# Output projection of block pairs in seven products instead of eight, with the branch projections as a stage of their own

## The chip, the core and the metric

The kernel runs on one core of a Trainium2 chip. The number that counts is the time of one execution on the device in microseconds; "before" is the median of three runs. Beside the runs there is one execution under the hardware profiler, from which all rows in this document come.

## What is computed

One encoder layer is applied to two sequences of 1024 tokens, x_prompt and x_sample, with shared weights and 1024 features. Sixteen learned meta tokens stand in front of each sequence as extra keys. Cut to what matters here:

```python
proj = h @ w_in                                   # queries, keys, values, gates of both branches
ya = window_attention(...) * silu(za)             # (tokens, 512)
yb = dense_attention(...) * silu(zb)              # (tokens, 512)
ua = ya @ w_ba                                    # (512, 1024)
ub = yb @ w_bb                                    # (512, 1024)
merged = sigmoid(ga) * ua + sigmoid(gb) * ub      # (tokens, 1024)
out = merged @ w_o                                # (1024, 1024)
y = layer_norm(ALPHA * h + out) * ln_g + ln_b
```

Everything is float32. The kernel gets there with a reduced format of TensorE: each operand is split into a rounded high part and the remainder, and a product is the sum of three matmuls, high by high, high by low and low by high.

## The kernel before

The 2048 tokens are 16 blocks of 128. The program runs in stages: keys, values and the first two gate columns; windowed attention; dense attention; the last two gate columns; and at the end one loop over the 16 blocks that does the branch projections, the merge, the output projection and the normalization. Attention outputs (`ysc`) and gates (`gsc`) lie in DRAM between the stages. The change touches the last loop and, a little, the gate stage ahead of it.

In that loop `branches(i)` multiplies the two attention outputs of block i with `wba` and `wbb`. `project` issues three matmuls of 128x512 for each 128 rows of a weight; a branch has 4 such rows and there are two column halves, so that is 48 matmuls. DVE multiplies each of the four results with its gate out of PSUM, POOL adds the two branches (`sg<-sg`), TensorE transposes the sum in 8 pieces of 128x128, ACT writes its high part (`mh`) and DVE its low part (`ml`). `finish(i - 1)` multiplies the previous block with `w_out`: 2 column halves, 8 rows each, 3 matmuls, so 48 again. DVE then adds ALPHA times the input (`xr<-xr,st`), takes `bn_stats` and `bn_aggr`, subtracts the mean and multiplies with the gain (`xr<-xr,mv,ln_gain`), computes the inverse root by nine tiny instructions on 128x1 tiles (`lny`, `lnh`, `lna`) and scales and shifts each half (`xr<-xr,lny,ln_bias`). Two DMAs write the block out.

What sets the order: every instruction is recorded by `Plan.record`, priced by `Plan.price` and put in order by `Plan.issue`, which takes for each engine the ready instruction with the lowest key. The prices and the delays between engines are one number per instruction and pair of engines; nothing in them makes one engine's instruction longer because another engine is at work. Each engine then runs its list strictly in that order and waits where an input is late. All DMAs stand in one queue, SP's. Since all instructions are issued in `Plan.issue`, all rows of the profile have line 278, and the tile's name tells what is what. PSUM has 8 banks of 128x512, given out in rings by tag: `sx` 3, `st` 2, `pj`, `o` and `tr` one each.

Of the kernel before, what the change touches and what calls it, by code (L numbers as in the profile page):

```python
# [282 lines left out]
def encoder(ctx, tc, d, out):  # L283
# [591 lines left out]
    raw = []
    wg = [load_weight(wp, w_in(GATE[2 + i]), KT, f"w{i}", (None, ptt)[WSUB[2 + i]]) for i in range(2)]
    x = kept_x(0)
    for i in range(2 * NT):
        nx = kept_x(i + 1) if i + 1 < 2 * NT else None
        for c in range(2):  # L880
            if i <= GSPLIT:
                gates(x, i, 2 + c, wg[c], ("pj", 1), wk, (ROPE_TAGS + (("rqs", 1),))[2 * i + c], raw)
            else:
                gates(x, i, 2 + c, wg[c], ("st", 2), wk)
        x = nx
        if i == GSPLIT:
# [6 lines left out]
            wd = pool("wd", 1, reuse_waits="tile")
            wk = pool("wk3", 2, reuse_waits="tile")
            stage = lambda: xp.tile([P, 4, P], F32, tag="xf", bufs=XF).rearrange("p c q -> p (c q)")
            wb = [weight(wd, d[n], 4, n) for n in ("wba", "wbb")]
            lnp = [wk.tile([P, D], F32, name=n, bufs=1) for n in ("ln_gain", "ln_bias")]
            pieces = [p for _, ps in wb for p in ps]
            wb = [u for u, _ in wb]
# [4 lines left out]
    for p in pieces:
        p()

    def load_y(i):
        y = x_tile()
        for b in range(2):
            load_x(ysc[b][i], y, 4 * b)  # L910
        sg = wk.tile([P, 4, 512], F32, tag="sg")
        for c in range(4):
            dma(sg[:, c], gsc[i][c])
        return y, sg

    y = load_y(0)
    wo = [load_weight(wp, d["w_out"][:, c * 512:(c + 1) * 512], KT, f"w{c}") for c in range(2)]
    for t, n in zip(lnp, ("ln_gain", "ln_bias")):
        dma(t, d[n].to_broadcast([P, D]))

    def branches(i, y, sg):

        mh, ml = (wk.tile([P, KT, P], F32R, tag="m" + e) for e in "hl")
        us = [bank("pj", 1), bank("o", 1), bank("sx", 3), bank("sx", 3)]
        for c in range(4):
            half, b = c // 2, c % 2
            project(us[c], [t[:, 4 * b:4 * b + 4] for t in y], wb[b], 4, half * 512, 512)
        for c in range(4):
            tt(out=sg[:, c], in0=us[c], in1=sg[:, c], op=ALU.mult)
        for half in range(2):  # L930
            m = sg[:, 2 * half]
            ptt(out=m, in0=m, in1=sg[:, 2 * half + 1], op=ALU.add)
            tr = bank("tr", 1) if half else bank("sx", 3)
            for c in range(4):
                nc.tensor.transpose(tr[:, c * P:(c + 1) * P], m[:, c * P:(c + 1) * P], ident)
            r = slice(4 * half, 4 * half + 4)
            tr = tr.rearrange("p (c q) -> p c q", c=4)
            act(mh[:, r], tr, AF.Copy)
            tt(out=ml[:, r], in0=tr, in1=mh[:, r].bitcast(F32), op=ALU.subtract)
        return mh, ml  # L940

    def finish(i, m):

        xr = wk.tile([P, D], F32, tag="xr")
        dma(xr, d["xtok"][i * P:(i + 1) * P])
        stats = wk.tile([P, 2, 6], F32, tag="stats")
        for c in range(2):
            pw = misc()
            project(pw, m, wo[c], KT, 0, 512)
            xc = xr[:, c * 512:(c + 1) * 512]  # L950
            nc.vector.scalar_tensor_tensor(out=xc, in0=xc, scalar=ALPHA, in1=pw, op0=ALU.mult, op1=ALU.add)
            nc.vector.bn_stats(out=stats[:, c], in_=xc)
        mv = wk.tile([P, 2], F32, tag="mv")
        nc.vector.bn_aggr(out=mv, in_=stats)
        nc.vector.tensor_scalar(out=mv[:, 1:2], in0=mv[:, 1:2], scalar1=1e-5, scalar2=None, op0=ALU.add)
        stt = nc.vector.scalar_tensor_tensor
        stt(out=xr, in0=xr, scalar=mv[:, 0:1], in1=lnp[0], op0=ALU.subtract, op1=ALU.mult)
        rstd = rsqrt(wk, mv[:, 1:2], 1, P, "ln")
        for c in range(2):
            cs = slice(c * 512, (c + 1) * 512)  # L960
            stt(out=xr[:, cs], in0=xr[:, cs], scalar=rstd, in1=lnp[1][:, cs], op0=ALU.mult, op1=ALU.add)
            dma(out[i // NT][0, (i % NT) * P:(i % NT + 1) * P, cs], xr[:, cs])

    done = None
    for i in range(2 * NT):
        m = branches(i, *y)
        if i + 1 < 2 * NT:
            y = load_y(i + 1)
        if i:
            finish(i - 1, done)  # L970
        done = m
    finish(2 * NT - 1, done)
# [44 lines left out]
```

## Time and profile before

| | us |
|---|---|
| median of 3 runs (lowest to highest) | 1812.28 (1812.25 to 1813.5) |
| the profiled execution's own time | 1811.3 |
| its span, first to last instruction | 1809.5 |
| TensorE (PE) busy | 1772.6 (98%) |
| VectorE (DVE) busy | 1149.9 (64%) |
| ScalarE (ACT) busy | 883.2 (49%) |
| GpSimd (POOL) busy | 249.8 (14%) |
| first matmul of the last loop starts at | 1430.35 |

All times in rows count from the span's start. "out<-in" gives the tile written and the tiles read; in a row of the timeline the second number is the duration, and "x2" merges two instructions that follow each other, whose joint time then stands there. PE busy is the time that matmuls were under way, and since they overlap, the distance from one start to the next is what one costs.

### The profile page before, as it was taken

To read this page: it belongs to the slowest core of one execution; us is meant where nothing else is said; L and a number is where in the kernel's file an instruction comes from. 1 tells how busy PE (TensorE), PEld (TensorE's weight loads), DVE (VectorE), ACT (ScalarE), POOL (GpSimd) and SP (SyncE) were. 2 spreads that over 40 slices of the span, in tenths; PEclk is the share of its full clock that TensorE was granted. 3 is DMA by queue.
4 is the path that set the end of the run, shared out by engine and by line. 5 is a ranking of instruction groups with operands and counts; after the bars stand their busy time and mean duration, and the time that the engine had idled before them with its cause. 6 is when DMAs were issued, how large, how long until landed. Compare 5 with 4: busy or idle time off the path is not lost. (4 is left out here: it accounts for less than half of the span.)

```text
span 1809.5 us, 26295 instructions
## 1 busy us (share of the span) xinstructions
PE 1772.6 (98%) x8954; PEld 1453.4 (80%) x8954; DVE 1149.9 (64%) x2908; ACT 883.2 (49%) x2265; POOL 249.8 (14%) x437
## 2 busy tenths in 40 slices
PE   7999999999999999999999999999999999999997
PEld 5778778888888778888888888877888878888886
DVE  7433334767677679888888888887200265555555
ACT  6222224666666667777777777788311220000000
POOL 2000002222221131111111111132000011111110
PEclk9999999999999999999999999999999999999999
DMA  9544445322223340100002000131654553333321
GB/s 338 215 161 163 141 145 182 124 92 91 95 96 99 103 143 32 56 30 33 30 33 76 30 33 30 41 103 59 241 180 155 186 169 117 117 117 116 111 71 47
DMA packets 111101, 199.09 MB, mean 110 GB/s; under 512 B 11814, under 2 KB 49894, under 8 KB 110966
## 3 DMA queue, kind: packets, MB, share of 16 engines
q1 hardware_dynamic: 110966, 197.40, 32.5%
q8 instruction: 71, 1.16, 0.3%
q14 instruction: 64, 0.52, 0.1%
HBM read 138.60 MB, written 58.75 MB: 109 GB/s over the span
## 5 line engine op out<-in xcount | busy, mean ns | idle before, releaser
L278 DVE TENSOR_TENSOR pl<-st,ph 116x512 fp32r<-116x512 f32 (+3 forms) x416 | 283.2, 684 | 56.1 <-ACT ph L278 52.1
L278 ACT ACTIVATE ph<-st 116x512 fp32r<-116x512 f32 (+3 forms) x416 | 248.1, 599 | 117.0 <-PE st L278 113.8
L278 PE MATMUL st<-ident,p 128*116 128x128 f32 (+2 forms) x1664 | 261.7, 272 | 6.4 <-ACT p L278 4.1
L278 PE MATMUL sx<-k,q 128*128 128x348 f32 (+3 forms) x1024 | 245.9, 340 | 5.2 <-ACT p L278 4.6
L278 PEld LDWEIGHTS st<-ident,p 128*116 128x116 f32 (+2 forms) x1664 | 200.8, 131 | 56.7 <-issue 7.7
L278 ACT ACTIVATE p<-sx,nb 128x348 f32<-128x348 f32 (+1 forms) x384 | 208.1, 552 | 56.1 <-DVE nb L278 55.9
L278 DVE TENSOR_REDUCE mn<-sx 128x1 f32<-128x348 f32 (+1 forms) x384 | 190.7, 511 | 34.4 <-PE sx L278 32.3
L278 PEld LDWEIGHTS sx<-k,q 128*128 128x128 f32 x1024 | 168.6, 189 | 34.5 <-ACT p L278 12.3
L278 PE MATMUL o<-ph,v 116*128 116x512 f32 (+3 forms) x416 | 179.3, 431 | 0.6 <-DVE yu L278 0.4
L278 ACT ACTIVATE xh<-xf 128x512 fp32r<-128x512 f32 x64 | 38.9, 626 | 287.8 <-PE sx L278 222.6
L278 PE MATMUL o<-pl,v 116*128 116x512 f32 (+3 forms) x416 | 167.0, 401 | 1.7 <-DVE pl L278 1.7
L278 DVE TENSOR_TENSOR xl<-xf,xh 128x512 fp32r<-128x512 f32 x64 | 57.2, 912 | 165.3 <-ACT xh L278 165.2
L278 PE MATMUL pj<-w0h,xh 128*128 128x512 f32 x272 | 112.9, 415 | 0.3 <-DVE z L278 0.3
L278 POOL TENSOR_TENSOR sg<-sg 128x512 f32<-128x512 f32 x32 | 46.2, 1445 | 469.0 <-DVE sg L278 276.2
L278 PE MATMUL pj<-w1h,xh 128*128 128x512 f32 x264 | 110.0, 417 | 0.5 <-DVE rope_rq L278 0.5
L278 PE MATMUL pj<-w0l,xh 128*128 128x512 f32 x272 | 107.9, 397 | 0.0
L278 PE MATMUL pj<-w1l,xh 128*128 128x512 f32 x264 | 107.3, 406 | 0.0
L278 PE MATMUL pj<-w0h,xl 128*128 128x512 f32 x272 | 107.0, 394 | 0.0
L278 PE MATMUL pj<-w1h,xl 128*128 128x512 f32 x264 | 106.4, 403 | 0.0
L278 ACT ACTIVATE q<-tr 64x256 fp32r<-64x256 f32 x256 | 96.4, 376 | 14.5 <-PE tr L278 11.8
L278 PEld LDWEIGHTS o<-pl,v 116*128 116x128 f32 (+3 forms) x416 | 78.8, 189 | 16.6 <-DVE pl L278 9.0
L278 PEld LDWEIGHTS o<-ph,v 116*128 116x128 f32 (+3 forms) x416 | 78.4, 188 | 14.5 <-ACT ph L278 5.4
(194 smaller groups left out, 3777.0 us busy)
## 6 DMA issues: line engine op xcount, KB each, us to landing
xh<-xsc SPq DMA_DIRECT2D x48, 512.0 KB
xl<-xsc SPq DMA_DIRECT2D x48, 512.0 KB
wf<-in_w_in_dram SPq DMA_DIRECT2D x64, 256.0 KB
gsc<-sg SPq DMA_DIRECT2D x64, 256.0 KB
sg<-gsc SPq DMA_DIRECT2D x64, 256.0 KB
xf<-in_xt_dram SPq DMA_DIRECT2D x32, 256.0 KB
xsc<-xh SPq DMA_DIRECT2D x16, 512.0 KB
xsc<-xl SPq DMA_DIRECT2D x16, 512.0 KB
```

What stands on the lines that cost most here:

```text
L278: getattr(op.eng.real, op.name)(*map(real, op.a), **{k: real(v) for k, v in op.k.items()})
```

## The change

The loop at the end becomes two stages.

The first stage goes over the 16 blocks twice, once for each half of the 1024 columns (`order`). `merge` does the two branch products of a block and a half (24 matmuls), multiplies with the gates, and adds the branches on DVE. `put_m`, two steps later, transposes the sum (4 pieces), copies it to SBUF unsplit and writes it to DRAM (`msc`). The attention outputs are read and split once for each half, so twice in all. Between these steps `operand` prepares seven combinations of the four quarters of `w_out` (quarters 11, 12, 21, 22 of 512x512): three quarters as they are and `t1 = 12 - 11`, `t2 = 22 - t1`, `t3 = 22 - 12`, `t4 = 21 - t2`. The differences are taken on POOL, and each result is split on ACT and DVE.

The second stage takes blocks in pairs, 2j and 2j + 1. Of the pair's merged block (2x2 pieces of 512 columns) `put` makes seven left operands: three pieces as they are and `s1 = 21 + 22`, `s3 = 11 - 21`, `s2 = s1 - 11`, `s4 = 12 - s2`, all four on POOL. Each operand is split: high part on ACT, low part on DVE, or on POOL for s2 and s4 (`SUBS`). `product` does one of the seven 512-deep products of a pair: 4 rows, 3 matmuls each, so 12 matmuls, and 84 for a pair where the loop before had 96. `put` runs `LEAD` = 4 products ahead. The products are put together on DVE (`e1`, `u2`, `u3`, `residual`), where `residual` also sums a row's values; `norm` takes the mean, lets ACT sum the squares, and scales and shifts on DVE. The seven products take seven of the eight PSUM banks in turn (`BANKS`). Gate tiles and other work tiles move to new rings (`raw`, 10 buffers; `xo`, 6).

TensorE has 768 matmuls of 128x512 less 96, so 672, in the output projection; the 768 of the branch projections and the 128 transposes stay as many.

```diff
+    def merge(h, y, sg):
+        us = [bank("sx", 3), bank("st", 2)]
+        for b in range(2):
+            project(us[b], [t[:, 4 * b:4 * b + 4] for t in y], wb[h][b], 4, 0, 512)
+            tt(out=sg[:, b], in0=us[b], in1=sg[:, b], op=ALU.mult)
+        m = sg[:, 0]
+        tt(out=m, in0=m, in1=sg[:, 1], op=ALU.add)
+        return m
...
+    def minus(x, y, o=None):
+        o = x if o is None else o
+        ptt(out=o, in0=x, in1=y, op=ALU.subtract)
+        return o
...
+    def put(o, n):
+        s = pairs[n]
+        if o == "11":
+            s.raw = {}
+            for q in ("11", "12", "21", "22"):
+                f = s.raw[q] = raw_tile()
+                r, c = int(q[0]) - 1, int(q[1]) - 1
+                dma(f, msc[2 * s.j + r][:, 4 * c:4 * c + 4])
+        f = s.raw
+        if o == "s3":
+            f["s1"] = raw_tile()
+            ptt(out=f["s1"], in0=f["21"], in1=f["22"], op=ALU.add)
+            f["s3"] = minus(f["11"], f["21"], f["21"])
+        elif o == "s2":
+            f["s2"] = minus(f["s1"], f["11"], f["11"])
+        elif o == "s4":
+            f["s4"] = minus(f["12"], f["s2"])
+        hl = wk.tile([P, 8, P], F32R, tag="xo", name="xo", bufs=XO)
+        act(hl[:, 0:4], f[o], AF.Copy)
+        (ptt if o in SUBS else tt)(out=hl[:, 4:8], in0=f[o], in1=hl[:, 0:4].bitcast(F32), op=ALU.subtract)
+        X[o, n] = hl[:, 0:4], hl[:, 4:8]
+
+    def product(o, n):
...
+        project(ps, X.pop((o, n)), (w_[:, 0:4], w_[:, 4:8]), 4, 0, 512)
+        if o == "11":
...
+            act(s.e1, ps, AF.Copy)
+        elif o == "12":
+            residual(s, 0, 0, ps, s.e1)
+        elif o == "s2":
+            s.u2, s.u3 = ev(), ev(False)
+            tt(out=s.u2, in0=ps, in1=s.e1, op=ALU.add)
+            tt(out=s.u3, in0=s.ps["s3"], in1=s.u2, op=ALU.add)
+        elif o == "22":
+            residual(s, 1, 0, ps, s.u3)
+        elif o == "s1":
+            tt(out=s.u2, in0=ps, in1=s.u2, op=ALU.add)
+            residual(s, 1, 1, ps, s.u3)
+            norm(s, 1)
+        elif o == "s4":
+            residual(s, 0, 1, ps, s.u2)
+            norm(s, 0)
+
+    def residual(s, r, c, src, more):
+        xc = flat(s.x[r][:, 4 * c:4 * c + 4])
+        nc.vector.scalar_tensor_tensor(out=xc, in0=xc, scalar=ALPHA, in1=src, op0=ALU.mult, op1=ALU.add)
+        nc.vector.tensor_tensor_reduce(out=xc, in0=xc, in1=more, op0=ALU.add, op1=ALU.add, scale=1.0, scalar=0.0,
+                                       accum_out=s.stats[r][:, c:c + 1])
+
+    def norm(s, r):
...
+        for c in range(2):
+            act(flat(raw_tile()), flat(xr[:, 4 * c:4 * c + 4]), AF.Square, bias=mv[:, 0:1], accum_out=sums[:, 2 + c:3 + c])
...
         rstd = rsqrt(wk, mv[:, 1:2], 1, P, "ln")
         for c in range(2):
             cs = slice(c * 512, (c + 1) * 512)
+            xc = flat(xr[:, 4 * c:4 * c + 4])
+            stt(out=xc, in0=xc, scalar=mv[:, 0:1], in1=lng[:, cs], op0=ALU.add, op1=ALU.mult)
+            stt(out=xc, in0=xc, scalar=rstd, in1=lnb[:, cs], op0=ALU.mult, op1=ALU.add)
```

How the lists of the engines read now, at two places. The first is POOL after the last attention step. Before, it has the 32 additions of the branches and nothing else, two for each block; the last five blocks:

```order
L278 TENSOR_TENSOR sg_18159<-sg_18159 128x512 x2
L278 TENSOR_TENSOR sg_18325<-sg_18325 128x512 x2
L278 TENSOR_TENSOR sg_18491<-sg_18491 128x512 x2
L278 TENSOR_TENSOR sg_18655<-sg_18655 128x512 x2
L278 TENSOR_TENSOR sg_18817<-sg_18817 128x512 x2
```

Now POOL has 28 differences for the weights in the first stage, and in the second stage, for each pair, these six instructions. They are shown for one pair in the middle, with buffer numbers; raw_19194 is s1, raw_19192 holds piece 21 and then s3, raw_19001 holds 11 and then s2, raw_19125 holds 12 and then s4:

```order
L280 TENSOR_TENSOR raw_19194<-raw_19192,raw_19193 128x512
L280 TENSOR_TENSOR raw_19192<-raw_19001,raw_19192 128x512
L280 TENSOR_TENSOR raw_19001<-raw_19194,raw_19001 128x512
L280 TENSOR_TENSOR raw_19125<-raw_19125,raw_19001 128x512
L280 TENSOR_TENSOR xo_19299<-raw_19001,xo_19299 128x512
L280 TENSOR_TENSOR xo_19386<-raw_19125,xo_19386 128x512
```

The additions `sg<-sg` moved to DVE, and six instructions of 128x512 for each pair of blocks took their place on POOL, where four stood for two blocks; each of the six has both inputs in SBUF.

The second place is DVE at the end of a block, and now at the end of a pair. Before, a block's mean, its inverse root and its last scaling stand like this, among the products with the gates:

```order
L278 SCALAR_TENSOR_TENSOR xr<-xr,st 128x512
L278 BN_STATS stats<-xr 128x6
L278 BN_AGGR mv<-stats 128x2
L278 TENSOR_SCALAR mv<-mv 128x1
L278 SCALAR_TENSOR_TENSOR xr<-xr,mv,ln_gain 128x1024
...
L278 TENSOR_SCALAR lny<-lny 128x1
L278 SCALAR_TENSOR_TENSOR lna<-lny,lnh 128x1
L278 SCALAR_TENSOR_TENSOR lny<-lna,lny 128x1
...
L278 SCALAR_TENSOR_TENSOR xr<-xr,lny,ln_bias 128x512 x2
L278 TENSOR_TENSOR sg<-o,sg 128x512
L278 TENSOR_TENSOR sg<-sx,sg 128x512 x2
L278 TENSOR_TENSOR ml<-sx,mh 128x512
```

Now (ISA is the instruction that adds and sums a row, and its read-out; xr_19082 is the pair's second block, xr_19111 its first, xr_19309 the next pair's first; raw_19199 and raw_19323 are pieces 11 and 12 of the pair after that; the last two rows are `u2` and `u3` of the next pair):

```order
L280 TENSOR_TENSOR xo_19406<-raw_19199,xo_19406 128x512
L280 SCALAR_TENSOR_TENSOR lny_19370<-lna_19377,lny_19370 128x1
...
L280 ISA xr_19309,stats0_19423<-xr_19309,ev_19364 128x512
...
L280 SCALAR_TENSOR_TENSOR xr_19082<-xr_19082,lny_19370,lnp_18368 128x512 x2
...
L280 TENSOR_TENSOR xo_19434<-raw_19323,xo_19434 128x512
L280 TENSOR_SCALAR lny_19440<-lny_19440 128x1
L280 SCALAR_TENSOR_TENSOR lna_19449<-lny_19440,lnh_19421 128x1
L280 SCALAR_TENSOR_TENSOR lny_19440<-lna_19449,lny_19440 128x1
...
L280 SCALAR_TENSOR_TENSOR xr_19111<-xr_19111,lny_19440,lnp_18368 128x512 x2
L280 TENSOR_TENSOR ev_19471<-sx_19431,ev_19364 128x512
L280 TENSOR_TENSOR ev_19480<-pj_19402,ev_19471 128x512
```

What was a block's tail between two products out of PSUM is now a run in which nearly every instruction reads two tiles of SBUF: splits for pairs further on, the sum, the scalings and the inverse roots of two blocks. The rows that read PSUM follow behind it.

More of the change, by code (lines that the diff above doesn't have):

```diff
@@ L35 @@
 GSPLIT = 1
+XO, RAWS, LEAD = 6, 10, 4
+SUBS = ("s2", "s4")
 DELAY = {
@@ L311, in encoder @@
     ysc = [[dram.tile([P, 4, P], F32, name=f"ysc{b}_{i}") for i in range(2 * NT)] for b in range(2)]
+    msc = [dram.tile([P, KT, P], F32, name=f"msc{i}") for i in range(2 * NT)]
     gsc = [[dram.tile([P, 512], F32, name=f"gsc{i}_{c}") for c in range(4)] for i in range(2 * NT)]
@@ L443, in gates @@
         project(pg, x, w, KT, 0, 512)
-        sg = pool_.tile([P, 512], F32, tag=tag[0], name="sg", bufs=tag[1])
+        sg = pool_.tile([P, 512], F32, tag=tag[0], name="sg", bufs=tag[1]) if tag else flat(raw_tile())
         def store(src=sg):
@@ L872, in encoder, with ev, split @@
     plan.key = 1e6
+    def ev(own=True):
+        return flat(xp.tile([P, 4, P], F32, tag="xf", name="ev", bufs=XF) if own else wk.tile([P, 4, P], F32, tag="ev", name="ev", bufs=3))
+    def split(t, k, src):
+        f = src
+        if not isinstance(src, View):
+            f = ev()
+            dma(f, src)
+        act(t[:, k], f, AF.Copy)
+        tt(out=t[:, 4 + k], in0=f, in1=t[:, k].bitcast(F32), op=ALU.subtract)
     raw = []
@@ L883, in encoder @@
             else:
-                gates(x, i, 2 + c, wg[c], ("st", 2), wk)
+                gates(x, i, 2 + c, wg[c], ("st", 2), wk, None)
         x = nx
@@ L892, in encoder @@
             ac_ctx.close()
[L893 to L899, printed above, removed]
+            op = pool("op", 1, reuse_waits="tile")
+            wk = pool("wk3", 1, reuse_waits="tile")
+            raw_tile = lambda: wk.tile([P, 4, P], F32, tag="raw", name="raw", bufs=RAWS)
+            flat = lambda t: t.rearrange("p c q -> p (c q)")
+            wb, pieces = [[], []], []
+            for h in range(2):
+                for b, n in enumerate(("wba", "wbb")):
+                    t = op.tile([P, 8, 512], F32R, tag=f"q{2 * h + b}", name="wb")
+                    wb[h].append((t[:, 0:4], t[:, 4:8]))
+                    pieces += [lambda t=t, n=n, h=h, k=k: split(t, k, d[n][k * P:(k + 1) * P, h * 512:(h + 1) * 512])
+                               for k in range(4)]
         if i > GSPLIT:
@@ L903, in encoder, with fetch_y @@
             pieces = pieces[2:]
[L904 to L908, printed above, removed]
+    def fetch_y(i, h):
+        y = [raw_tile() for b in range(2)]
         for b in range(2):
-            load_x(ysc[b][i], y, 4 * b)
-        sg = wk.tile([P, 4, 512], F32, tag="sg")
-        for c in range(4):
[L913 to L946, printed above, removed]
-        for c in range(2):
[L948 to L957, printed above, removed]
+            dma(y[b], ysc[b][i])
@@ new lines, in fetch_y, with fetch_sg, split_y @@
+        return y
+    def fetch_sg(i, h):
+        sg = wk.tile([P, 2, 512], F32, tag="xo", name="sg", bufs=XO)
+        for b in range(2):
+            dma(sg[:, b], gsc[i][2 * h + b])
+        return sg
+    def split_y(t, raw):
+        y = [wk.tile([P, KT, P], F32R, tag="xo", name="y", bufs=XO) for e in "hl"] if t % 3 == 2 else x_tile()
+        for b in range(2):
+            r = slice(4 * b, 4 * b + 4)
+            act(y[0][:, r], raw[b], AF.Copy)
+            tt(out=y[1][:, r], in0=raw[b], in1=y[0][:, r].bitcast(F32), op=ALU.subtract)
+        return y
@@ new lines, in merge, with put_m @@
+    def merge(h, y, sg):
+        us = [bank("sx", 3), bank("st", 2)]
+        for b in range(2):
+            project(us[b], [t[:, 4 * b:4 * b + 4] for t in y], wb[h][b], 4, 0, 512)
[3 more added lines that the diff above has]
+        return m
+    def put_m(i, h, m):
+        tr = bank("tr", 1)
+        for c in range(4):
+            nc.tensor.transpose(tr[:, c * P:(c + 1) * P], m[:, c * P:(c + 1) * P], ident)
+        f = raw_tile()
+        act(flat(f), tr, AF.Copy)
+        dma(msc[i][:, 4 * h:4 * h + 4], f)
@@ new lines, in encoder, with quarter, operand, t2 @@
+    W = {}
+    def quarter(r, c, k):
+        f = ev(False) if (r, c) == (2, 2) else flat(raw_tile())
+        dma(f, d["w_out"][((r - 1) * 4 + k) * P:((r - 1) * 4 + k + 1) * P, (c - 1) * 512:c * 512])
+        return f
+    def minus(x, y, o=None):
+        o = x if o is None else o
+        ptt(out=o, in0=x, in1=y, op=ALU.subtract)
+        return o
+    def operand(o, k):
+        def t2():
+            t1 = minus(quarter(1, 2, k), quarter(1, 1, k))
+            return minus(quarter(2, 2, k), t1)
+        if k == 0:
+            pool_, tag = WHERE[o]
+            W[o] = (op if pool_ else wp).tile([P, 8, 512], F32R, tag=tag, name="wo", bufs=1)
+        if o == "t1":
+            f = minus(quarter(1, 2, k), quarter(1, 1, k))
+        elif o == "t2":
+            f = t2()
+        elif o == "t3":
+            x = quarter(2, 2, k)
+            f = minus(x, quarter(1, 2, k))
+        elif o == "t4":
+            t = t2()
+            f = minus(quarter(2, 1, k), t)
+        else:
+            f = quarter(int(o[0]), int(o[1]), k)
+        split(W[o], k, f)
@@ new lines, in encoder @@
+    WHERE = {"11": (0, "w0h"), "21": (0, "w0l"), "t3": (0, "w1h"), "t1": (0, "w1l"), "t4": (1, "q0"), "t2": (1, "q1"), "22": (1, "q2")}
+    todo = [[(o, k) for o in ("11", "21", "t3", "t1") for k in range(4)], [(o, k) for o in ("t2", "t4") for k in range(4)]]
+    order = [(i, h) for h in range(2) for i in range(2 * NT)]
+    ys = [split_y(t, fetch_y(*order[t])) for t in range(2)]
+    raws = fetch_y(*order[2])
+    sg = fetch_sg(*order[0])
+    last = []
+    for t, (i, h) in enumerate(order):
+        m = merge(h, ys.pop(0), sg)
+        if len(last) > 1:
+            put_m(*last.pop(0))
+        if t + 1 < len(order):
+            sg = fetch_sg(*order[t + 1])
+        if t + 2 < len(order):
+            ys.append(split_y(t + 2, raws))
+        if t + 3 < len(order):
+            raws = fetch_y(*order[t + 3])
+        last.append((i, h, m))
+        for _ in range((i % 3 < 2 and i < 12) if h else 0 if i < 2 else 2 if i < 4 else 1):
+            operand(*todo[h].pop(0))
@@ new lines, in encoder @@
+    lnp = op.tile([P, 8, 512], F32R, tag="q3", name="lnp").bitcast(F32)
+    lng, lnb = (lnp[:, 2 * c:2 * c + 2].rearrange("p c q -> p (c q)") for c in range(2))
+    pairs = [SimpleNamespace(j=j, ps={}) for j in range(NT)]
+    PW = {"11": "11", "12": "21", "s3": "t3", "s2": "t2", "22": "t4", "s1": "t1", "s4": "22"}
+    seq = []
+    BANKS = (("sx", 3), ("st", 2), ("pj", 1), ("sx", 3), ("st", 2), ("o", 1), ("sx", 3))
+    for n in range(NT):
+        seq += [(o, n) for o in PW]
+    X = {}
+    def put(o, n):
[19 more added lines that the diff above has]
+        X[o, n] = hl[:, 0:4], hl[:, 4:8]
@@ new lines, in product @@
+    def product(o, n):
+        s = pairs[n]
+        t = 7 * n + list(PW).index(o)
+        ps = s.ps[o] = bank(*BANKS[t % 7])
+        w_ = W[PW[o]]
+        project(ps, X.pop((o, n)), (w_[:, 0:4], w_[:, 4:8]), 4, 0, 512)
+        if o == "11":
+            s.x = [xp.tile([P, KT, P], F32R, tag=t, name="xr").bitcast(F32) for t in ("xh", "xl")]
+            for r in range(2):
+                dma(s.x[r], d["xtok"][(2 * s.j + r) * P:(2 * s.j + r + 1) * P].rearrange("p (c q) -> p c q", q=P))
+            s.stats = [wk.tile([P, 4], F32, tag=f"stats{r}", bufs=2) for r in range(2)]
+            s.e1 = ev()
+            act(s.e1, ps, AF.Copy)
[14 more added lines that the diff above has]
+            norm(s, 0)
@@ new lines, in residual @@
+    def residual(s, r, c, src, more):
[4 more added lines that the diff above has]
+    def norm(s, r):
+        xr, i = s.x[r], 2 * s.j + r
+        stt = nc.vector.scalar_tensor_tensor
+        mv = wk.tile([P, 2], F32, tag="mv", bufs=2)
+        sums, ts = s.stats[r], nc.vector.tensor_scalar
+        ts(out=mv[:, 0:1], in0=sums[:, 0:1], scalar1=sums[:, 1:2], scalar2=-1.0 / D, op0=ALU.add, op1=ALU.mult)
+        for c in range(2):
+            act(flat(raw_tile()), flat(xr[:, 4 * c:4 * c + 4]), AF.Square, bias=mv[:, 0:1], accum_out=sums[:, 2 + c:3 + c])
+        tt(out=mv[:, 1:2], in0=sums[:, 2:3], in1=sums[:, 3:4], op=ALU.add)
+        ts(out=mv[:, 1:2], in0=mv[:, 1:2], scalar1=1.0 / D, scalar2=1e-5, op0=ALU.mult, op1=ALU.add)
@@ L960, in finish @@
             cs = slice(c * 512, (c + 1) * 512)
[L961 to L972, printed above, removed]
+            xc = flat(xr[:, 4 * c:4 * c + 4])
+            stt(out=xc, in0=xc, scalar=mv[:, 0:1], in1=lng[:, cs], op0=ALU.add, op1=ALU.mult)
+            stt(out=xc, in0=xc, scalar=rstd, in1=lnb[:, cs], op0=ALU.mult, op1=ALU.add)
+            dma(out[i // NT][0, (i % NT) * P:(i % NT + 1) * P, cs], xc)
+    for m in last:
+        put_m(*m)
+    for t in range(LEAD):
+        put(*seq[t])
+    for t, o in enumerate(seq):
+        if t == 2:
+            for k in range(4):
+                operand("22", k)
+            for t_, n in ((lng, "ln_gain"), (lnb, "ln_bias")):
+                dma(t_, d[n].to_broadcast([P, D]))
+        if t + LEAD < len(seq):
+            put(*seq[t + LEAD])
+        product(*o)
     plan.issue()
```

## The prediction

> **What bounds the kernel now.** I read the page's totals first, then busy time by stretches of 50 us, then the chain of work that ended last.
>
> ```profile
> span 1809.5 us, 26295 instructions
> PE 1772.6 (98%) x8954; PEld 1453.4 (80%) x8954; DVE 1149.9 (64%) x2908; ACT 883.2 (49%) x2265; POOL 249.8 (14%) x437
> ```
>
> In the stretches the numbers behind the second are the busy us of each engine, then the granted clock, the DMA engines' share and GB/s.
>
> ```profile
> 0.00:250.00 250.00, 240.91 (x1032) 187.15 (x1033) 113.22 (x408) 77.64 (x162) 22.26 (x54) 1.00 0.57 200
> 1600.00:1650.00 50.00, 49.94 (x228) 40.83 (x227) 27.83 (x54) 4.47 (x8) 5.92 (x4) 1.00 0.37 122
> ```
>
> In the last loop PE is busy throughout at full clock, DVE a little over half the time. The chain confirms it. One block there, and the end:
>
> ```profile
> 1686.46 2.07 PE st L278 x9
> 1689.21 8.87 PE st L278 x39
> 1698.08 2.72 PE pj L278 x12
> 1700.80 2.72 PE o L278 x12
> 1703.52 5.88 PE sx L278 x28
> 1709.40 2.07 PE st L278 x9
> ...
> 1800.28 0.70 DVE xr L278
> ...
> 1804.95 0.75 DVE xr L278
> ```
>
> ```profile
> 1430.35 0.39 PE L278 MATMUL pj<-wbah,xh 128*128 128x512 f32 x1
> ```
>
> Twelve matmuls take 2.72 us, 0.2267 each. A block takes 1709.40 - 1686.46 = 22.94 us: 96 matmuls (21.76) and 8 transposes, 0.59 for four. The loop begins at 1430.35 and PE is done at 1800.28, 369.9 us, of which 16 x 22.94 = 367.0 are work. Whatever removes matmuls here removes time, as long as the other engines keep up.
>
> **What the change removes.** 96 matmuls, 96 x 0.2267 = 21.8 us of PE. The first stage's 768 matmuls and 30 groups of transposes last 174.1 + 17.7 = 191.8 us, to 1430.35 + 191.8 = 1622.2; a pair's seven products last 84 x 0.2267 = 19.05 us. So the question is whether DVE and POOL can finish a pair in 19.05 us.
>
> **What a pair costs DVE.** What counts on DVE is the distance between starts; durations overlap.
>
> ```profile
> 1462.06 0.68 DVE L278 TENSOR_TENSOR xl<-xf,xh 128x512 fp32r<-128x512 f32 x1
> 1462.66 0.15 DVE L278 SCALAR_TENSOR_TENSOR lny<-lna,lny 128x1 f32<-128x1 f32 x1
> 1462.85 0.22 DVE L278 SCALAR_TENSOR_TENSOR lna<-lny,lnh 128x1 f32<-128x1 f32 x1
> ...
> 1465.34 1.41 DVE L278 SCALAR_TENSOR_TENSOR xr<-xr,lny,ln_bias 128x512 f32<-128x512 f32 x2
> 1466.67 0.68 DVE L278 TENSOR_TENSOR sg<-sx,sg 128x512 f32<-128x512 f32 x1
> ```
>
> ```profile
> 1803.24 0.14 DVE L278 TENSOR_SCALAR lny<-mv 128x1 int32<-128x1 int32 x1
> ...
> 1804.95 1.42 DVE L278 SCALAR_TENSOR_TENSOR xr<-xr,lny,ln_bias 128x512 f32<-128x512 f32 x2
> ```
>
> ```profile
> L278 DVE CUSTOM_DVE_ANT_0 p<-sx,mask 128x400 f32<-128x400 f32 x96 | 52.8, 567 | 6.5 <-PE sx L278 6.2
> L278 DVE CUSTOM_DVE_ANT_0 p<-sx,mask 128x272 f32<-128x272 f32 x32 | 13.4, 431 | 5.0 <-PE sx L278 5.0
> ```
>
> A 128x512 operation takes 0.60 (1462.06 to 1462.66), the scaling of a half 0.66 (1465.34 to 1466.67 for two), an inverse root by itself 1.71 for nine tiny rows (1803.24 to 1804.95). The summing instruction of `residual` is not there with 512 columns; by 567 and 431 ns for 400 and 272 columns it would last 0.69, and less the usual overlap of 0.07 I take 0.62. A pair has 7 rows that read PSUM (4.2), 5 splits (3.0), 4 sums (2.5), 8 scalings (5.3), two inverse roots and six more tiny rows, partly between the large ones (3.5), and 0.2 where a row waits for the one ahead: 18.7 us, 98% of PE's 19.05, with nothing yet in its way.
>
> **What POOL puts in its way.** POOL has six instructions of 128x512 a pair. These rows show what one does to DVE, first DVE's, then POOL's:
>
> ```profile
> 1201.18 0.53 DVE L278 TENSOR_TENSOR rqa<-rqy 128x8 f32<-128x8 f32 x1
> 1201.74 1.22 DVE L278 SCALAR_TENSOR_TENSOR rqa<-rqa,rqms 128x8 f32<-128x8 f32 x1
> ...
> 1463.77 1.34 DVE L278 SCALAR_TENSOR_TENSOR lna<-lny,lnh 128x1 f32<-128x1 f32 x1
> ...
> 1660.40 0.69 DVE L278 TENSOR_TENSOR sg<-sx,sg 128x512 f32<-128x512 f32 x1 [0.94 <-PE sx L278]
> 1663.73 2.38 DVE L278 TENSOR_TENSOR xl<-xf,xh 128x512 fp32r<-128x512 f32 x2
> ```
>
> ```profile
> 1200.40 2.53 POOL L278 TENSOR_TENSOR w0l<-wf,w0h 128x512 fp32r<-128x512 f32 x2 [1.25 <-ACT w0h L278]
> ...
> 1463.80 1.29 POOL L278 TENSOR_TENSOR sg<-sg 128x512 f32<-128x512 f32 x1 [20.30 <-DVE lny L278]
> ...
> 1659.60 1.29 POOL L278 TENSOR_TENSOR sg<-sg 128x512 f32<-128x512 f32 x1 [16.98 <-DVE sg L278]
> 1663.89 1.67 POOL L278 TENSOR_TENSOR sg<-sg 128x512 f32<-128x512 f32 x1 [3.00 <-DVE sg L278]
> ```
>
> An operation out of PSUM runs at its 0.69 under a POOL addition (1660.40). Two splits, which read two tiles of SBUF, take 2.38 instead of 1.29 beside one POOL addition, and that one 1.67 instead of 1.29. A 128x1 row of two SBUF inputs, 0.22 elsewhere, takes 1.34: until POOL's addition is over. Between two POOL operations in a row one DVE row gets through and the next waits again (0.53, then 1.22). So one POOL operation costs DVE up to its 1.25 us (2.53 for two), unless a row from PSUM is next. The two splits alone would allow another reading, that both engines share a port at part speed; then the tiny row should not have suffered. [...]
>
> Six times 1.25 is 7.5 us. What can lie beside it free of charge is 4.2 of PSUM rows and some 2.1 of one-input rows and gaps of dependent ones. So a pair loses between 7.5 - 6.3 = 1.2 and 7.5. Random placement would cover a third. By the order, s1 and s3 wait for the load of pieces 21 and 22, whose buffers come free only when POOL has split s4 of the pair ahead; s2 and s4 follow at once, and that meets the run of splits, scalings and inverse roots at the end of a pair, where between the split of piece 12 and `u2` no PSUM row stands and eight rows, one after the other, can be held up. I take 0.95 each, 5.7 us, and 24.4 us a pair: DVE bounds the second stage, and PE waits some 5 us a pair for banks.
>
> **The rest.** What stays hidden is ACT:
>
> ```profile
> L278 ACT ACTIVATE xh<-xf 128x512 fp32r<-128x512 f32 x64 | 38.9, 626 | 287.8 <-PE sx L278 222.6
> ```
>
> With 8 copies and 4 sums of squares a pair it is busy for about 12 x 0.65 = 8 of 24 us. On SP, the loads for later pairs stand behind a pair's four writes, which wait for DVE's last scaling; a late DVE delays them, but they are wanted a pair later. In the first stage, for a half of 6.03 us (24 matmuls and 4 transposes), DVE has five to six operations, 3.4 us, and POOL one of 1.25 on average. Its DMAs are many:
>
> ```profile
> sg<-gsc SPq DMA_DIRECT2D x64, 256.0 KB
> xf<-in_w_out_dram SPq DMA_DIRECT2D x16, 256.0 KB
> ```
>
> Each half moves five pieces of 256 KB, the weights another 52: 212 x 0.262 MB = 55.6 MB in 191.8 us, 290 GB/s, where 200 GB/s filled 0.57 of the engines, so 351 would fill them. I allow 1.5 us of stalls. If the cover fails, that is the fourth rival.
>
> **The sum.** First stage to 1622.2. The first `residual` comes after two products and the last two groups of transposes, 2 x 2.72 + 1.2: 1628.8. DVE then has 8 x 18.7 less the five splits of pair 0, done by then: 146.6, to 1775.4. POOL's hold over seven pairs, 7 x 5.7 = 39.9, to 1815.3. The last pair has nothing to put between its sums and scalings (1.5, an estimate: two sums of squares on ACT by the row above), and the last write lands as now, 1809.5 - (1804.95 + 1.42) = 3.1: 1819.9, with the stalls 1821.4. The profiled execution's own time is 1.8 above its span (1811.3), and the median 1.0 above that: **1824**, 0.65% slower. Break-even is where 1775.4 + 7B + 6.1 = 1809.5, B = 4.0 us a pair, 0.67 for each POOL operation.
>
> **The rivals.**
>
> *POOL's six mostly fall beside PSUM rows* (place: `u2`, `u3` and the three residuals behind each other, 1.9 and 1.2 us). If the loads land some 6 us later in the pair than I think, s1 to s4 meet that run. At 2.5 us a pair: 1775.4 + 17.5 + 6.1 = 1799.0, run 1802, faster. It decides from B below 4. For it: the PSUM rows follow right behind the run. Against: they cover two of six operations.
>
> *PE stays the bound*, DVE's rows being closer together than I price them: 1622.2 + 1.2 + 672 x 0.2267 = 1775.7, some 8 us for the last block's sums, squares, inverse root and scalings, 3.1: 1786.8, run 1790. Against it: 18.7 + 1.2 is over 19.05 already.
>
> *Ports shared at part speed:* only large two-input rows suffer, 10.8 of 18.7 us. A POOL operation then lasts 1.67 and takes 0.6 of that time from them: 6 x 1.67 x 0.58 x 0.6 = 3.5 a pair, 1775.4 + 24.5 + 6.1 = 1806, run 1809, no change.
>
> *The first stage falls behind too:* where `t4` is made, three halves move 23 pieces in 18.1 us, 333 GB/s, and two of the three have three POOL differences and six DVE operations, 3.75 + 3.6 us against 6.03. At 12 us lost in all, run 1835.
>
> **How the numbers follow.** My forecast 0.54, the fourth rival 0.09, no change (the third, or B near 4) 0.11, the first 0.21, the second 0.05. A difference under 0.2% (3.6 us) can't be told from none here. Slower 0.63, same 0.11, faster 0.26. The forecast's own range, B from 4.6 to 7, is 1816 to 1833. To leave out no more than two in ten, the range goes down into the first rival and up over the fourth: 1798 to 1838.
>
> **What would show it.** Right: in the second stage PE waits for DVE (`ev`, `xr`) at bank after bank, a pair takes 23 to 26 us, DVE is busy over 90%, and `lna`, `xo` and `xr` rows of over 1.2 us lie beside POOL's `raw` rows; the first stage shows PE at 49 of 50 us. Wrong: pairs of 19 to 21 us with PE full (first or second rival), tiny rows that are not held up under POOL (third), or PE waiting already before 1622 (fourth).

## The result, and the profile after

The changed kernel takes 1824.14 us, the kernel before 1812.89 us on the same chip: 1.0066 times the time, with a 95% interval of 1.0054 to 1.0078. It is slower, as forecast, and by the amount forecast (1824); that the amount fits to the microsecond is luck in part, since errors cancel in it, as the part on what offset what shows. The page after, its span and its engines:

```profile
span 1821.7 us, 26890 instructions
PE 1759.2 (97%) x8858; PEld 1440.0 (79%) x8858; DVE 1252.8 (69%) x3080; ACT 966.8 (53%) x2437; POOL 316.1 (17%) x481
```

PE is busy 13.4 us less than before (1772.6 to 1759.2), of the 21.8 us removed; the rest shows as matmuls that last longer behind PE's waits (ten in 3.94 and 4.07 us instead of 2.57, twelve in 5.74 and 5.49 instead of 2.88), on which the last section says more. The span is 12.2 us longer all the same (1809.5 to 1821.7). The stretches say why. Columns: busy time of each engine, then the granted clock, the DMA engines' share and GB/s.

```profile
1450.00:1500.00 50.00, 50.00 (x239) 41.37 (x238) 33.98 (x50) 19.00 (x34) 5.89 (x4) 1.00 0.81 271
1500.00:1550.00 50.00, 50.00 (x237) 41.30 (x236) 37.51 (x51) 18.53 (x34) 13.69 (x10) 1.00 0.95 326
1675.00:1700.00 25.00, 20.29 (x81) 15.78 (x80) 24.55 (x54) 7.40 (x16) 9.34 (x8) 0.93 0.39 126
1700.00:1725.00 25.00, 21.44 (x81) 16.70 (x81) 24.27 (x53) 7.39 (x16) 9.07 (x7) 0.86 0.38 127
1725.00:1750.00 25.00, 22.53 (x99) 18.04 (x98) 24.55 (x54) 7.40 (x16) 9.43 (x7) 1.00 0.38 127
```

In the first stage PE is full, even where the DMA engines are 0.95 busy. In the second DVE is full (24.3 to 24.6 of 25) and PE is not. One pair on DVE, from one `u3` (`ev<-pj,ev`) to the next, with the rows that stand out, and POOL beside it:

```profile
1711.31 0.69 DVE L280 TENSOR_TENSOR ev<-pj,ev 128x512 f32<-128x512 f32 x1
...
1720.26 0.22 DVE L280 SCALAR_TENSOR_TENSOR lna<-lny,lnh 128x1 f32<-128x1 f32 x1
1720.52 0.16 DVE L280 SCALAR_TENSOR_TENSOR lny<-lna,lny 128x1 f32<-128x1 f32 x1
...
1722.12 1.27 DVE L280 SCALAR_TENSOR_TENSOR lny<-lna,lny 128x1 f32<-128x1 f32 x1
...
1723.37 0.67 DVE L280 SCALAR_TENSOR_TENSOR xr<-xr,st 128x512 f32<-128x512 f32 x1
1723.97 0.67 DVE L280 SCALAR_TENSOR_TENSOR lna<-lny,lnh 128x1 f32<-128x1 f32 x1
...
1725.16 1.23 DVE L280 SCALAR_TENSOR_TENSOR lny<-lna,lny 128x1 f32<-128x1 f32 x1
...
1726.99 2.43 DVE L280 SCALAR_TENSOR_TENSOR xr<-xr,lny,lnp 128x512 f32<-128x512 f32 x2
...
1730.32 1.34 DVE L280 SCALAR_TENSOR_TENSOR lna<-lny,lnh 128x1 f32<-128x1 f32 x1
1731.69 1.22 DVE L280 SCALAR_TENSOR_TENSOR lny<-lna,lny 128x1 f32<-128x1 f32 x1
...
1733.84 1.41 DVE L280 SCALAR_TENSOR_TENSOR xr<-xr,lny,lnp 128x512 f32<-128x512 f32 x2
...
1735.88 0.69 DVE L280 TENSOR_TENSOR ev<-pj,ev 128x512 f32<-128x512 f32 x1
```

```profile
1721.58 1.78 POOL L280 TENSOR_TENSOR xo<-raw,xo 128x512 fp32r<-128x512 f32 x1 [13.27 <-issue]
1723.33 4.87 POOL L280 TENSOR_TENSOR raw<-raw 128x512 f32<-128x512 f32 x3
1730.35 1.29 POOL L280 TENSOR_TENSOR raw<-raw 128x512 f32<-128x512 f32 x1 [2.15 <-issue]
1731.60 1.29 POOL L280 TENSOR_TENSOR xo<-raw,xo 128x512 fp32r<-128x512 f32 x1
```

The pair takes 1735.88 - 1711.31 = 24.57 us. Rows of 128x1 that read two SBUF tiles and last 0.16 or 0.22 alone last up to 1.34 while POOL is at work (one 0.67, the others 1.22 to 1.34), and two scalings last 2.43 instead of 1.41. The row out of PSUM (`xr<-xr,st` at 1723.37) takes its usual 0.67 under POOL. What the held rows last beyond their usual lengths (0.16, 0.22, 0.16, 1.41, 0.22, 0.16) adds up to 1.11 + 0.45 + 1.07 + 1.02 + 1.12 + 1.06 = 5.83 us. PE's side, in the pair before this one and at the start of this one:

```profile
1687.20 0.70 PE L280 MATMUL pj<-wo,xo 128*128 128x512 f32 x2 [3.87 <-DVE ev L280]
1688.31 3.94 PE L280 MATMUL pj<-wo,xo 128*128 128x512 f32 x10 [0.40 <-DVE xo L280]
...
1705.71 2.88 PE L280 MATMUL st<-wo,xo 128*128 128x512 f32 x12
1712.15 5.74 PE L280 MATMUL pj<-wo,xo 128*128 128x512 f32 x12 [3.56 <-DVE ev L280]
```

PE's long wait is one a pair, at the single bank `pj`, until `u3` has read it.

### The profile page after: what moved, and what is told of

Same layout as the page of the kernel before. It is cut to its first block, busy times and chain, and to the rows that moved or that the text cites. A ratio compares the mean times of both kernels' runs of the same rounds, so it can differ in the third digit from the quotient of the medians.

```text
span 1821.7 us, 26890 instructions
## 1 busy us (share of the span) xinstructions
PE 1759.2 (97%) x8858; PEld 1440.0 (79%) x8858; DVE 1252.8 (69%) x3080; ACT 966.8 (53%) x2437; POOL 316.1 (17%) x481
## 5 line engine op out<-in xcount | busy, mean ns | idle before, releaser
L280 PEld LDWEIGHTS sx<-k,q 128*128 128x128 f32 x1024 | 168.4, 189 | 34.6 <-ACT p L280 12.5
L280 ACT ACTIVATE p<-p,nb 128x400 f32<-128x400 f32 (+1 forms) x128 | 75.8, 594 | 26.4 <-DVE nb L280 26.1
L280 POOL TENSOR_TENSOR raw<-raw 128x512 f32<-128x512 f32 x44 | 64.5, 1466 | 101.8 <-DMA raw<-in_w_out_dram 25.3
L280 POOL MEMSET q<- 64x512 f32 x64 | 33.3, 521 | 272.3 <-PE sx L280 229.9
```

Source lines behind the costliest of these rows:

```text
L280: getattr(op.eng.real, op.name)(*map(real, op.a), **{k: real(v) for k, v in op.k.items()})
```

## The experiments

The theory: while a POOL instruction that reads SBUF is at work, a DVE instruction with two SBUF inputs stands still, as the 128x1 row of 1.34 us (0.22 elsewhere) in the prediction, and six of them a pair make DVE the bound. The rivals: DVE's own new rows are too many, whatever POOL does; POOL's results come late and others wait for them; both engines read at part speed, the prediction's third rival; any POOL work disturbs. Times of 1 run are read beside spans and pairs; ratios come with their interval. Line 280 in the rows is the line of `Plan.issue` that issues every instruction, so rows are told apart by their tiles. The kernel before had a median of 1811.6 us beside four of the runs (without POOL's six, memsets, splits on DVE, all six on DVE) and 1813.3 beside the other four.

### Without POOL's six instructions

```diff
-            f["s1"] = raw_tile()
-            ptt(out=f["s1"], in0=f["21"], in1=f["22"], op=ALU.add)
-            f["s3"] = minus(f["11"], f["21"], f["21"])
+            f["dummy"] = raw_tile()
+            f["s1"], f["s3"] = f["22"], f["21"]
...
-            f["s2"] = minus(f["s1"], f["11"], f["11"])
+            f["s2"] = f["11"]
...
-            f["s4"] = minus(f["12"], f["s2"])
+            f["s4"] = f["12"]
...
+        if o in SUBS:
+            X[o, n] = hl[:, 0:4], hl[:, 0:4]
+            return
```

> Left out: POOL's six instructions of each pair in the second stage. The raw pieces stand in for s1 to s4, and the high part of the s2 and s4 operands is used in the low part's place, so PE, ACT, the DMAs and DVE's own rows stay as many. Theory (POOL's instructions hold up DVE's rows that read two SBUF tiles, 5.9 us a pair): DVE falls back to its 18.7 us a pair, PE's 19.05 bound again, span 1787 to 1793. Rival (DVE's rows by themselves take 24.6 us a pair, and POOL has no part in it): no change, span 1821. Rival (both share a port at part speed, 3.5 us of the 5.9): with the 3.5 gone, 21 us a pair, span about 1797.

Measured: 1788.06 us, span 1786.3, just under the 1787 to 1793 expected. One stretch of the second stage:

```profile
1700.00:1725.00 25.00, 25.00 (x112) 20.71 (x111) 24.31 (x73) 11.00 (x24) 0.00 (x0) 1.00 0.38 128
```

PE is full, the clock is 1.00, and a pair takes 19.05 us (`u3` at 1672.82 and 1691.87). All of DVE's rows (3080, as in the changed kernel) but none of POOL's six are here, and from 1640 to 1760 no 128x1 row lasts more than 0.22 us, so DVE's own rows alone are not what makes the kernel slow. This is also the floor that PE sets for this design. It does not tell yet whether POOL's work or the wait for its results costs the time.

### POOL reads, and nobody waits for it

The kernel above, with six additions on POOL that read two tiles each and write a tile that nobody reads:

```diff
             f["s1"], f["s3"] = f["22"], f["21"]
+            nc.gpsimd.tensor_tensor(out=f["dummy"], in0=f["21"], in1=f["22"], op=ALU.add)
+            nc.gpsimd.tensor_tensor(out=f["dummy"], in0=f["11"], in1=f["21"], op=ALU.add)
... (two more each for "s2" and "s4")
```

> As the run without POOL's six instructions (their results left out in the same way: raw pieces for s1 to s4, the high part for the low one of s2 and s4), plus six additions of 128x512 a pair on POOL that read two tiles of SBUF and whose results nobody uses. Nothing waits for POOL's results here, so what is lost is what POOL's reading alone does to DVE. By the lock (a DVE row with two SBUF inputs stands still while POOL's instruction lasts): pair 23 to 25 us as in the changed kernel, PE waiting again, 1813 to 1826 us. If the loss of the changed kernel came from waits for POOL's results (s1 to s4 or the two low parts coming late): pair 19.05 us, PE full, 1787 to 1791 us.

Measured: 1822.7 us, span 1820.9. The stretch, then DVE and POOL in one place:

```profile
1700.00:1725.00 25.00, 21.61 (x87) 17.02 (x86) 24.55 (x53) 7.29 (x16) 9.97 (x7) 0.93 0.38 127
```

```profile
1687.38 0.68 DVE L280 TENSOR_TENSOR ev<-pj,ev 128x512 f32<-128x512 f32 x1
...
1696.17 1.84 DVE L280 SCALAR_TENSOR_TENSOR xr<-xr,mv,lnp 128x512 f32<-128x512 f32 x1
1697.94 1.25 DVE L280 SCALAR_TENSOR_TENSOR lna<-lny,lnh 128x1 f32<-128x1 f32 x1
...
1699.85 1.24 DVE L280 SCALAR_TENSOR_TENSOR lny<-lna,lny 128x1 f32<-128x1 f32 x1
...
1712.04 0.68 DVE L280 TENSOR_TENSOR ev<-pj,ev 128x512 f32<-128x512 f32 x1
```

```profile
1696.18 9.86 POOL L280 TENSOR_TENSOR raw<-raw 128x512 f32<-128x512 f32 x6 [13.32 <-DMA raw<-msc]
```

The pair is back at 1712.04 - 1687.38 = 24.66 us, and the time within 1.5 us of the changed kernel's. Nobody reads what these additions write, and DVE is full (24.55 of 25), so a wait for POOL's results is not needed for the loss: these six additions alone bring all of it. The six held rows of this pair exceed their usual lengths by 5.89 us, which leaves 18.77 for DVE's own rows, as the changed kernel's 18.74. Six additions a pair move the time by 1822.7 - 1788.1 = 34.6 us, of which 1.7 may be the two batches, since the kernel before differs by that much between them.

### POOL writes only; POOL copies

Two more forms in the same place: twelve memsets a pair (`nc.gpsimd.memset(flat(f["dummy"]), 0.0)`, four at each of the three places), and six copies (`nc.gpsimd.tensor_copy(out=f["dummy"], in_=f["21"])` and so on).

> The kernel without POOL's six instructions, with twelve memsets of 128x512 for each pair on POOL instead: they write SBUF and read nothing. At 0.52 us each (the memset of 64x512) that is 6 us of POOL a pair, nearly as much as the six took. Theory that POOL holds DVE up through the read side that both use: as without POOL, span 1787 to 1793. Rival that any POOL instruction holds DVE up: near the changed kernel again, span 1812 to 1822.

> The same with six copies of 128x512 a pair on POOL (one SBUF input) in place of the six additions. If the lock takes any POOL instruction that reads SBUF: DVE is held as long as the copies last, so pair over 19.05 us by six times about the copy's length less what is covered, 1800 to 1826 us. If only POOL instructions with two inputs hold DVE: pair 19.05 us, 1787 to 1791 us, as with the memsets.

Measured: 1789.07 us with the memsets and 1794.78 with the copies. With the memsets:

```profile
1650.00:1675.00 25.00, 25.00 (x112) 20.72 (x111) 24.09 (x67) 9.01 (x18) 22.58 (x43) 1.00 0.52 179
```

The order had bunched most of the memsets into the first 50 us of the stage, so POOL is busy for 22.58 of 25 us here, and PE stays full. DVE's 67 instructions are busy for 24.09 us in this stretch; in the same stretch of the run without POOL's six there are 67 too, busy for 23.97. The 0.12 between them is small beside the 5.83 that six reading instructions hold DVE for, so POOL's being busy, and its writing, are not what holds it up. With the copies, a place where they run, DVE and then POOL:

```profile
1685.58 1.10 DVE L280 SCALAR_TENSOR_TENSOR xr<-xr,mv,lnp 128x512 f32<-128x512 f32 x1
1686.61 0.56 DVE L280 SCALAR_TENSOR_TENSOR lna<-lny,lnh 128x1 f32<-128x1 f32 x1
...
1687.83 0.56 DVE L280 SCALAR_TENSOR_TENSOR lny<-lna,lny 128x1 f32<-128x1 f32 x1
```

```profile
1684.74 5.51 POOL L280 COPY raw<-raw 128x512 f32<-128x512 f32 x6 [14.74 <-DMA raw<-msc]
```

Two of the six, each by itself:

```profile
1686.21 0.95 POOL L280 COPY raw<-raw 128x512 f32<-128x512 f32 x1
1687.22 1.16 POOL L280 COPY raw<-raw 128x512 f32<-128x512 f32 x1
```

Rows are held here too, for less time: 0.56 instead of 0.16 or 0.22. They end when the copy ends (1686.61 + 0.56 = 1687.17 and 1686.21 + 0.95 = 1687.16; 1687.83 + 0.56 = 1688.39 and 1687.22 + 1.16 = 1688.38). A pair takes 20.25 us (`u3` at 1676.79 and 1697.04) on DVE, and the time lies between the two that were expected, because a copy is shorter than an addition (5.51 us for six against 9.86) and holds a row by 0.34 to 0.40 us instead of about 1.05. The four rows held in this pair exceed their usual lengths by 1.50 us, and 20.25 - 1.50 = 18.75 is once more what DVE's own rows take. PE does not wait in this run (25.00 of 25 in 1700 to 1725); DVE falls behind it by 1.2 us a pair, which lengthens the end. Additions with two SBUF inputs hold a 128x1 row to 1.24 or 1.25 us, copies with one to 0.56, until the copy is over; beside memsets, which read nothing, DVE is busy for 24.09 us where it is 23.97 without them. What in the chip holds the rows, no run shows.

### What one instruction on POOL costs more than on DVE

Three kernels with all the work in them: the two splits on DVE, the sum and the differences on DVE, all six on DVE.

```diff
-SUBS = ("s2", "s4")
+SUBS = ()
```

```diff
-            ptt(out=f["s1"], in0=f["21"], in1=f["22"], op=ALU.add)
-            f["s3"] = minus(f["11"], f["21"], f["21"])
+            tt(out=f["s1"], in0=f["21"], in1=f["22"], op=ALU.add)
+            f["s3"] = f["21"]
+            tt(out=f["s3"], in0=f["11"], in1=f["21"], op=ALU.subtract)
... (s2 and s4 in the same way)
```

The splits (first edit):

> The low parts of the s2 and s4 operands are taken on DVE instead of POOL (SUBS is empty); the four differences stay on POOL. Theory: each POOL instruction costs DVE about 0.98 us a pair and by itself would cost it 0.60, so two moved save 0.76 a pair, 5.3 us over seven pairs: span 1816, ratio to the kernel before 1.0035. Rival (DVE's own rows alone): 1.2 us a pair more, span 1830, ratio 1.011.

The sum and the differences (second edit):

> Only the sum and the three differences go to DVE; POOL keeps the two splits. With six on POOL a pair took 24.57 us, with four 23.43, with none 20.7. By the lock each instruction on POOL costs about the same, (24.57 - 20.7) / 6 = 0.65 more than on DVE: pair 22.0 us, 1806 to 1811 us. If the four differences were what costs (they come in one run, s1, s3, s2): pair 20.7 to 21.2 us, 1799 to 1803 us. If DVE's tiny rows were held by the splits alone: 22.5 us or more, over 1811 us.

All six (both edits):

> All six instructions of a pair (four differences, two splits) go to DVE; POOL has nothing in the second stage. Theory: DVE takes 18.7 + 6 x 0.60 = 22.3 us a pair instead of 24.6, span 1821.7 - 16 = 1806, ratio to the kernel before 0.998. Rival (DVE's own rows alone): 3.6 us a pair more, span 1847, ratio 1.02. Rival (ports shared at part speed, 3.5 us a pair lost): 3.5 for 3.6, no change, span 1822.

Measured, with the distance between two `u3` rows as the pair:

| on POOL | pair, us | held, us | moved to DVE, us | other rows, us | time, us | ratio to before (95%) |
|---|---|---|---|---|---|---|
| six (the change) | 24.57 | 5.83 | 0 | 18.7 | 1824.14 | 1.0066 (1.0054 to 1.0078) |
| four (splits on DVE) | 23.43 | 3.88 | 1.2 | 18.4 | 1816.36 | 1.0029 (1.0018 to 1.0040) |
| two (differences on DVE) | 21.8 to 21.9 | 1.67 | 2.4 | 17.8 | 1807.71 | one run |
| none (all on DVE) | 20.7 | 0 | 3.6 | 17.1 | 1799.18 | 0.9932 (0.9915 to 0.9948) |

"Held" is what the held rows of one pair last beyond their usual lengths, "moved" is 0.60 for each instruction that DVE took over. Moving instructions from POOL to the engine that is the bound makes the kernel faster at each step. Span 1815.3 with the splits moved and a pair of 21.9 with the sum and the differences moved are what the theory expected (1816 and 22.0). The two splits bring (24.57 - 23.43) / 2 = 0.57 each, the sum and the differences (24.57 - 21.85) / 4 = 0.68, so neither kind is the culprit alone. Over six it is (24.57 - 20.7) / 6 = 0.65 an instruction, and two things make it up: 0.97 of hold against 0.60 of work on DVE, which is 0.37, and 0.27 because the other rows got shorter too.

With all six on DVE I had expected a span of 1806 and got 1797.8. Those other rows are why:

```profile
1695.37 0.68 DVE L280 TENSOR_TENSOR ev<-pj,ev 128x512 f32<-128x512 f32 x1
1695.97 0.21 DVE L280 SCALAR_TENSOR_TENSOR lna<-lny,lnh 128x1 f32<-128x1 f32 x1
1696.09 0.69 DVE L280 TENSOR_TENSOR raw<-raw 128x512 f32<-128x512 f32 x1
1696.70 0.15 DVE L280 SCALAR_TENSOR_TENSOR lny<-lna,lny 128x1 f32<-128x1 f32 x1
1696.76 0.68 DVE L280 SCALAR_TENSOR_TENSOR xr<-xr,st 128x512 f32<-128x512 f32 x1
```

Here a tiny row costs 0.06 to 0.13 us between two large ones, and about 0.19 when the chain runs by itself (the 1.71 us for nine in the prediction). With more large rows at hand, more of the tiny ones are interleaved: 20.7 less six times 0.60 leaves 17.1 us for the rest, not the 18.7 of a pair whose inverse root runs by itself.

### All six on DVE, one inverse root for two blocks

```diff
-            norm(s, 1)
+            if n == NT - 1:
+                norm(s, 1)
...
-            norm(s, 0)
+            norm(s, *((1, 0) if n < NT - 1 else (0,)))
...
-        rstd = rsqrt(wk, mv[:, 1:2], 1, P, "ln")
+        rstd = rsqrt(wk, mv[:, 2:2 + k], k, P, f"ln{k}")
```

Here `k` is the number of blocks whose roots are taken together, one column each.

> All six on DVE as in the run that was faster than both kernels, and the two blocks of a pair share one inverse root (one chain of eleven tiny rows of 128x2 for two chains of nine rows; the last pair keeps two). DVE is what bounds there, at 20.7 us a pair. If each tiny row costs DVE its issue of 0.1 to 0.15 us: seven rows less and a shared scaling, pair 19.7 to 20.2 us, 1791 to 1796 us, ratio 0.989 to 0.992. If the tiny rows only fill gaps that other rows leave: no gain, 1798 to 1800 us. If the first block's scalings, now later, crowd the end of the pair: over 1800 us.

Measured: 1796.39 us, ratio 0.9911 (0.9895 to 0.9928), span 1795.2: near the first of the three, though the pair came out just under its range and the time just over. It beats both kernels, but its interval overlaps that of the run before, so the gain over that one is not settled. Six pairs take 117.6 us (`u3` from 1656.32 to 1773.90, 19.6 each), without the edit 123.8 (1654.00 to 1777.8, 20.6 each): 6.2 us less. The span is only 2.6 us shorter. The rest is given back at the two ends: the pair ahead of these takes 22.5 us (1633.79 to 1656.32) against 20.8 (1633.19 to 1654.00) and starts 0.6 later, and from the last `u3` to the end of the span it is 21.3 us against 20.0.

## Why the prediction was right, point by point

**PE is not what bounds.** Right. Where POOL's six are left out, or POOL only writes, PE is full and the kernel takes 1788 to 1789 us, which is the second rival's 1790. With POOL at its work it fell, as the prediction had it.

**DVE's own 18.7 us and POOL's 5.7.** Right in both terms: in the quoted pair the excess of the held rows is 5.83 us, and 24.57 - 5.83 = 18.74 is left, with 18.77 and 18.75 in the runs with additions that nobody reads and with copies. The mean over five pairs is 24.69 (1661.64 to 1785.07), where 24.4 was the forecast. The 18.7 is not a fixed price, though; it holds for this order of rows, and falls to 17.1 where large rows stand between the tiny ones.

**Where POOL's instructions fall.** Right in the main: the split of s4 of the pair ahead and then s1, s3 and s2 in one run (1721.58 to 1728.2), s4 and the split of s2 from 1730.35, on the inverse roots and one of the scalings, with one PSUM row under them; so each costs 5.83 / 6 = 0.97, and I took 0.95. No split (`xo`) is held in this pair, though I had named such rows. The first rival (PSUM rows cover most of it) would have needed several. One-input rows of 128x1, part of the cover, are not held: four of them (`mv<-mv`, `lny<-mv`, `lnh<-mv`, `lny<-lny`) last 0.14 or 0.15 us from 1645.43 on, under POOL's split of 1644.94 to 1646.66. It is not so for every one-input row: in the kernel before, `rqy<-rqms` of 128x8 took 0.99 us at 652.15 beside a POOL split, and 0.17 at 1197.54 with POOL at rest. That the buffers of the loads are what fixes this place was argued only: no run changed it.

**Rows that stand still, not part speed.** Right. By the third rival only large rows suffer, and a 128x1 row lasted 1.27 us (0.16 elsewhere); a pair would have been 3.5 us longer than 18.7, not 5.8.

**The first stage.** Right that it keeps up: PE is full in 1450 to 1600 at 271 to 326 GB/s, so the fourth rival fell, and of the 1.5 us allowed for stalls a wait of 0.47 shows. That the last transposes run at 1621.64 to 1622.27, where I had 1622.2, is luck: ten matmuls of the first product (2.3 us) had run ahead of them, and the stage itself is shorter than I priced it, as the next point says.

**What offset what.** The span came out at 1821.7 against 1821.4, with three errors in it that cancel; that is luck. Two groups of transposes on PE, one half of the first stage apart, and then rows of the second stage on DVE:

```profile
1605.97 0.60 PE L280 MATMUL tr<-ident,sg 128*128 128x128 f32 x4
...
1611.89 0.60 PE L280 MATMUL tr<-ident,sg 128*128 128x128 f32 x4
```

```profile
1625.50 0.69 DVE L280 SCALAR_TENSOR_TENSOR xr<-xr,st 128x512 f32<-128x512 f32 x1 [0.86 <-PE st L280]
...
1631.66 0.69 DVE L280 TENSOR_TENSOR ev<-pj,ev 128x512 f32<-128x512 f32 x1
...
1661.64 0.69 DVE L280 TENSOR_TENSOR ev<-pj,ev 128x512 f32<-128x512 f32 x1
...
1785.07 0.69 DVE L280 TENSOR_TENSOR ev<-pj,ev 128x512 f32<-128x512 f32 x1
...
1803.87 0.69 DVE L280 TENSOR_TENSOR ev<-pj,ev 128x512 f32<-128x512 f32 x1
...
1817.16 1.41 DVE L280 SCALAR_TENSOR_TENSOR xr<-xr,lny,lnp 128x512 f32<-128x512 f32 x2
```

The first `residual` came at 1625.50, 3.3 us before my 1628.8. PE had all that I counted to do before it, but a half took 5.92 us (1605.97 to 1611.89) and not the 6.03 of the sum, some 3 us over thirty halves, and the stage began 0.6 us earlier, at 1429.71. I had priced a group of transposes at the 0.59 that a block before leaves for it; here 5.92 less 24 matmuls (5.44) leaves 0.48.

From there DVE took until its last scalings were done, 193.1 us (1625.50 to 1818.57), where the sum had 188.0 (1628.8 to 1816.8), seven equal pairs of 24.4 among them. The first pair lasts 29.98: POOL has eleven instructions in it, which hold DVE for 7.9 us, and DVE waits 3.1 for ACT and PE. The last step lasts 18.80, since POOL has a single split left there (1.84 us at 1795.29). These two cancel. What is left of the 5.1 are 1.4 us in the five pairs between, at 24.69 each, and 3.7 us ahead of the first `u3` and behind the last, where DVE took 20.9 and the sum had 17.2. With the 1.5 us of stalls that did not come, that is -3.3 + 5.1 - 1.5 = +0.3.

**How PE's waits look.** Wrong in detail: not bank after bank but one bank a pair. `pj` has one buffer and is read last, by `u3`; behind it the other banks are free.

## What to carry to other kernels

Before work is given to an idle engine, ask what it does to the engine that is nearly full: here six POOL instructions with SBUF inputs held DVE for 0.97 us each, more than the 0.60 that DVE needs for the same work, and leaving POOL idle turned a loss of 0.7% into a gain of 0.7%. Tiny rows show such a hold best, because a 128x1 row of 1.2 us that lasts 0.16 or 0.22 elsewhere cannot be explained by its own work. A run in which the suspected engine does the same work for nobody tells contention from waiting for its results.

## What the runs showed of the hardware that was not expected

The granted clock of TensorE fell behind some of PE's waits. After a wait of 3.56 us the next twelve matmuls took 5.74 us instead of 2.88 (1712.15), and the clock was 0.50 from 1712.15 to 1717.70 (0.86 in the whole stretch). After a wait of 2.06 us at 1736.72 it stayed at 1.00 (two matmuls, and ten in 2.57 us behind a further 0.40):

```profile
1736.72 0.70 PE L280 MATMUL pj<-wo,xo 128*128 128x512 f32 x2 [2.06 <-DVE ev L280]
1737.83 2.57 PE L280 MATMUL pj<-wo,xo 128*128 128x512 f32 x10 [0.40 <-DVE xo L280]
```

With the splits on DVE, matmuls behind two waits of nearly the same length differ:

```profile
1687.77 2.56 PE L280 MATMUL pj<-wo,xo 128*128 128x512 f32 x10 [2.36 <-DVE xo L280]
...
1711.20 3.98 PE L280 MATMUL pj<-wo,xo 128*128 128x512 f32 x10 [2.40 <-DVE xo L280]
```

Ten matmuls take 2.56 us after 2.36 us of waiting and 3.98 after 2.40, and PE had been at work for 8.4 us without a break ahead of the second (1700.34 to 1708.79). So the length of the wait alone does not tell when the clock falls; what does, no run here shows. Nothing shows that the lower clock cost time in this kernel, since DVE was busy for 24.3 to 24.6 of 25 us all the while; what it costs where PE is the bound, no run here shows.
